# A two-layer decoder trunk: squares on ScalarE, earlier sums, another product order and spread loads in its MLPs

## The chip, the cores and the metric

The kernel runs on one core of a Trainium2 chip. The metric is the device time of one execution in microseconds (us), as the median of several runs. The profile is of one execution and has its own time, given below. Engines are named as in the profile: PE is TensorE's matmul, PEld its weight load, DVE is VectorE, ACT is ScalarE, POOL is GpSimd, SP (SPq for its queue) is SyncE, which issues the DMAs.

## The reference

One sequence of 512 positions, width 1024, two layers. Layer 0 mixes with a gated spatial unit and latent attention (the even mixer), layer 1 with gated linear attention (the odd mixer). The change is in the MLP, which both layers have:

```python
def sqrelu_mlp(x, w1, w2):
    return jnp.square(jax.nn.relu(x @ w1)) @ w2
# per layer, with d = 1024 and D_FF = 4096, everything float32
x = layer_norm(ALPHA * x + mixer(x), ln1_g[layer], ln1_b[layer])
x = layer_norm(ALPHA * x + sqrelu_mlp(x, w_ff1[layer], w_ff2[layer]), ln2_g[layer], ln2_b[layer])
```

## The kernel before

Each float32 operand of a matmul is held as two fp32r parts: `hi` is a cast by ACT, `lo` is what is left, a subtraction by DVE (`split`, L163 to L165). A product is three matmuls: hi by hi, hi by lo, lo by hi.

The MLP is `ff`. Its hidden width of 4096 is cut into eight groups of 2 x 256 columns (the group number is `g`, NG = 8). Group 0 is computed by eight plain block products (`plain`). Groups 1 to 7 use Strassen's scheme in Winograd's form: seven products of half-size blocks (`product`, named P1, p3, p5, p7, p6, P2, p4 in the order in which they run), with sums of blocks of x (s1 to s4, made once per layer in `x_sums`) and sums of blocks of w1 (t1 to t4, made for every group by `sum1`). A product has 24 matmuls of 256 columns.

The results of the seven products are combined by DVE (V, X and the blocks C11, C12, C21, C22; the table of steps L483 to L489), and each block passes `relu2`: relu and square by ACT, then twice DVE, then it lies in `hq[g]` as `hh` and `hl`. The second matrix is applied by chunk (`ff2_half`, chunk c takes `hq[c]`): eight halves, each with 12 matmuls of 512 columns, and each added into `XN` by DVE (`add_half`, L208). The last two chunks, 6 and 7, are the closing (`close_blocks` in layer 0, `close_final` in layer 1), which also does the layer norm; in layer 0 `norms` transposes a finished block of x (`block_T`, L194) while the next is computed.

The order on PE is: group 0, chunk 0, groups 1 and 2 one behind the other, chunk 1, group 3, chunk 2, and so on to group 7, then the closing. PE and DVE run their instructions in the order in which the program writes them (`manual_schedule`, `in_order`). The order on ACT and on SP is made by the framework's scheduler when the kernel is built.

Weights come in the order of the list `wseq`. `upto(n)` issues the loads and then the splits and sums ("terms") of all entries before place n. Ahead of each product and each half it runs a few places in front of what PE needs. Buffers that matter: `cr` (two, raw blocks B11 and B12, in which t1, t2, t4 and t3 are summed in place), `xk` (one, which holds the transposed x of the second half of the positions until its sums are made, and then B22 and B21 of a group), `raw` (three, for w2 and the next mixer's weights), six PSUM banks taken in turn, of which a group takes five and a half of a chunk one.

After the last group the next mixer's first weights are loaded: `prefetch` is `load_v0`, four granules (L129 to L140: a DMA, a cast by ACT, a subtraction by DVE at L138).

Of the kernel before, what the change touches and what calls it, by code (L numbers as in the profile page):

```python
# [12 lines left out]
F32 = mybir.dt.float32  # L13
F32R = mybir.dt.float32r
I32 = mybir.dt.int32
U8 = mybir.dt.uint8
AF = mybir.ActivationFunctionType
ALU = mybir.AluOpType

P = 128  # L20
D = 1024
# [82 lines left out]
def trunk(ctx: ExitStack, tc: tile.TileContext, a: dict, out: bass.AP):  # L104
    nc = tc.nc
# [19 lines left out]
    def bank(name, tag=None):  # L125
        tag = tag or next(cycle)
        return ps.tile([P, 512], F32, tag=tag, name=name, bufs=BANKS[tag])

    def granule(src, kb, cols, pool=wp, raw=None):  # L129

        n = kb * cols
        if raw is None:
            raw = wp.tile([P, WG], F32, tag="raw", name="raw", bufs=3)
        hi = pool.tile([P, WG], F32R, tag="whi", name="whi")
        lo = pool.tile([P, WG], F32R, tag="wlo", name="wlo")
        nc.sync.dma_start(raw[:, :n].rearrange("p (k c) -> p k c", k=kb), src.rearrange("(k p) c -> p k c", p=P))
        nc.scalar.copy(hi[:, :n], raw[:, :n])  # L137
        nc.vector.tensor_tensor(lo[:, :n], raw[:, :n], hi[:, :n].bitcast(F32), ALU.subtract)  # L138
        v = lambda x: x[:, :n].rearrange("p (k c) -> p k c", k=kb)
        return v(hi), v(lo)  # L140
# [14 lines left out]
    def granules(w, r0, rows, kb, cols, pool=wp):  # L155
        return [granule(w[r:r + kb * P, cols], kb, cols.stop - cols.start, pool) for r in range(r0, r0 + rows, kb * P)]
# [6 lines left out]
    def split(hi, lo, src):  # L163
        nc.scalar.copy(hi, src)  # L164
        nc.vector.tensor_tensor(lo, src, hi.bitcast(F32), ALU.subtract)  # L165
# [113 lines left out]
    HALF_S, HK_, GF = S // 2, KD // 2, 2 * P  # L279
# [4 lines left out]
    def ff(layer, hp, fp, xp, out_proj, prefetch):  # L284

        w1, w2 = a["w_ff1"][layer], a["w_ff2"][layer]
# [5 lines left out]
        ops = {"A11": (XH[:, lo_k, lo_t], XL[:, lo_k, lo_t]), "A12": (XH[:, hi_k, lo_t], XL[:, hi_k, lo_t]),  # L292
               "A22": (XH[:, hi_k, hi_t], XL[:, hi_k, hi_t]), "s1": (XH[:, lo_k, hi_t], XL[:, lo_k, hi_t])}
        xr, kept = {}, []
        ops["A21"] = ops["s1"]

        def operand(n, t, src, which=(0, 1)):
            h, l = (z[:, :, (t % 2) * P:(t % 2 + 1) * P] for z in ops[n])
            src = src.rearrange("p (k c) -> p k c", k=HK_)
            if 0 in which:  # L300
                nc.scalar.copy(h, src)
            if 1 in which:
                nc.vector.tensor_tensor(l, src, h.bitcast(F32), ALU.subtract)
# [17 lines left out]
        def x_lo(t):  # L321
            for h in range(2):
                operand(f"A{1 + t // 2}{1 + h}", t, xr[t, h], (1,))

        def x_sums():

            for n in ("s2", "s3", "s4"):
                ops[n] = (xp.tile([P, HK_, HALF_S], F32R, tag=n + "h", name="sh"),
                          xp.tile([P, HK_, HALF_S], F32R, tag=n + "l", name="sl"))
            for n, x, y, op in (("s3", (0, 0), (2, 0), ALU.subtract), ("s1", (2, 1), (2, 0), ALU.subtract),  # L330
                                ("s2", (0, 0), (2, 1), ALU.add), ("s4", (2, 1), (0, 1), ALU.subtract)):
                for t in range(2):
                    i, j = xr[x[0] + t, x[1]], xr[y[0] + t, y[1]]

                    to = i if n == "s3" else j
                    nc.vector.tensor_tensor(to, i, j, op)
                    operand(n, t, to)
                yield

        ff_T["now"] = x_T  # L340
# [6 lines left out]
        SUM = {"t1": ("B11", "B12"), "t3": ("B12", "B22"), "t2": ("t1", "B22"), "t4": ("t2", "B21")}  # L347

        def load1(g, n):

            for m in (n,) if g == 0 else {"B11": ("B11", "B12"), "B21": ("B21",), "B22": ("B22",)}.get(n, ()):
                if g == 0 and m != "B22":
                    raw = wp.tile([P, WG], F32, tag="raw", name="raw", bufs=3)
                elif g == 0 or m in ("B11", "B12"):
                    raw = xp.tile([P, WG], F32, tag="cr", name="cr", bufs=2)
                else:
                    if g not in kept2:
                        kept2[g] = xp.tile([P, 2, WG], F32, tag="xk", name="cr2")
                    raw = kept2[g][:, m == "B21"]
                raws[g, m] = raw  # L360
                nc.sync.dma_start(raw.rearrange("p (k c) -> p k c", k=HK_), w1v(*BLOCK[m], g))
# [32 lines left out]
        def load2(c, n, half):  # L394
            r = half * 2048 + c * GF
            raw = wp.tile([P, WG], F32, tag="raw", name="raw", bufs=3)
            nc.sync.dma_start(raw.rearrange("p (k c) -> p k c", k=2),
                              w2[r:r + GF, n * 512:(n + 1) * 512].rearrange("(k p) c -> p k c", p=P))
            raws["w2", c, n, half] = raw
# [13 lines left out]
        def scratch(g):  # L413

            return fp.tile([P, S], F32, name="r", **({"tag": "x", "bufs": 4} if g and next(turns) == "x" else {"tag": "q"}))

        def relu2(g, i, j, src, into=None):
            hh = hp.tile([P, 2, HALF_S], F32R, tag="hh", name="hh")
            hl = hp.tile([P, 2, HALF_S], F32R, tag="hl", name="hl")
            r = into if into is not None else scratch(g)  # L420
            f = lambda z: z.rearrange("p j t -> p (j t)")
            nc.scalar.activation(r, src, AF.Relu)
            nc.scalar.activation(f(hh), r, AF.Square)  # L423
            nc.vector.tensor_tensor(r, r, r, ALU.mult)  # L424
            nc.vector.tensor_tensor(f(hl), r, f(hh).bitcast(F32), ALU.subtract)  # L425
            hq[g][i, j] = hh, hl

        banks, state = {}, {}
# [12 lines left out]
        def plain(i, j, k):  # L441

            hq.setdefault(0, {})
            if k == 0:
                banks[0, i, j] = bank("f1")
            mul(banks[0, i, j], f"A{i + 1}{k + 1}", got_w[0, f"B{k + 1}{j + 1}"], k == 0)
            if k == 1:
                relu2(0, i, j, banks[0, i, j])
# [49 lines left out]
            add_half(t, n, acc, c == 0, None)  # L498


        LATER = ("P1", "p3", "p5", "p7", "p6", "P2", "p4")
        slots, wseq = [], []

        def put_group(g):
            slots.extend((g, n) for n in LATER)
            wseq.extend((g, n) for n in ("B11", "B22", "t1", "t3", "t2", "B21", "t4"))

        def put_chunk(c):
            slots.extend(("w2", c, n, t) for n in range(2) for t in range(NT))
# [7 lines left out]
            put_chunk(c)  # L517
        put_group(NG - 1)
        wseq += [("w2", c, n, h) for n in range(2) for c in (NG - 2, NG - 1) for h in range(2)]
        place = {w: i for i, w in enumerate(wseq)}  # L520
        at = {"load": 0, "terms": 0}
        LOADS, TERMS = 6, 6

        def upto(n, loads=None):

            while at["load"] < min(len(wseq), n + (LOADS if loads is None else loads)):
                w = wseq[at["load"]]
                at["load"] += 1
                (load2(*w[1:]) if w[0] == "w2" else load1(*w))
            while at["terms"] < min(len(wseq), n):  # L530
                w = wseq[at["terms"]]
                i = at["terms"]
                at["terms"] += 1
                if i + 1 < at["load"] and wseq[i + 1][0] != "w2":
                    sum1(*wseq[i + 1])
                (terms2(*w[1:]) if w[0] == "w2" else terms1(*w))

        todo = 0
        for _ in out_proj:
            todo += 1  # L540
            upto(min(todo, 4), 2)
        for n, (i, j, k) in enumerate(itertools.product(range(2), repeat=3)):
            upto(min(8, 4 + max(0, n - 1)))
            plain(i, j, k)
            if n == 1:
                x_T(NT - 1)
                x_lo(NT - 2)
                x_lo(NT - 1)
        sums = x_sums()
        for i, s in enumerate(slots):  # L550
            if s[0] == "w2":
                need = max(place["w2", s[1], s[2], 1], place["w2", s[1], s[2], 0])
# [8 lines left out]
            product(*s)  # L561
        upto(len(wseq))
        load_ln(a["ln2_g"][layer], a["ln2_b"][layer])
        got = prefetch() if prefetch else None

        def close_mm(t, n, acc, o, m, k0, k1):
            i, tc_ = t // 2, slice(t % 2 * P, (t % 2 + 1) * P)
# [17 lines left out]
        def close_blocks():  # L585
            stats, accs = new_stats(), {}

            def mm(t, n, k0, k1):
                if k0 == 0:
                    accs[n] = bank("f2")  # L590
                close_mm(t, n, accs[n], 0, 512, k0, k1)
                if k1 == KD:
                    add_half(t, n, accs[n], False, stats)

            for _ in norms(mm, stats):
                pass

        (close_final if layer == DEPTH - 1 else close_blocks)()
        return got
# [671 lines left out]
        return steps  # L1271

    v0_cols = 2 * C_HEADS * C_DK
    load_v0 = lambda: granules(a["w_in_odd"][0], 0, D, 2, slice(v0_cols, v0_cols + 512))
    with tc.tile_pool(name="m0", bufs=1) as mp:
        left = even_mixer(mp)
        with in_order():
# [47 lines left out]
```

## Time and profile before

| what | value |
|---|---|
| median of 3 runs (lowest, highest) | 1194.95 us (1194.72, 1195.26) |
| the profiled execution: its time | 1197.36 us |
| the profiled execution: its span, first to last instruction | 1195.7 us |
| PE busy | 1155.0 us, 97% of the span |
| PEld busy | 1006.0 us, 84% |
| DVE busy | 872.6 us, 73% |
| ACT busy | 482.5 us, 40% |
| mean granted TensorE clock | 0.987 |
| matmuls | 6888 |

The shares are means over the span, and matmuls are pipelined with modelled ends, so a PE that is busy at 97% can still lose time: a matmul that runs at the lower clock counts as busy. What an engine waited for is in the view of waits, and the length of a stage is read from where its first and last matmul lie.

### The profile page before, as it was taken

To read this page: it belongs to the slowest core of one execution; us is meant where nothing else is said; L and a number is where in the kernel's file an instruction comes from. 1 tells how busy PE (TensorE), PEld (TensorE's weight loads), DVE (VectorE), ACT (ScalarE), POOL (GpSimd) and SP (SyncE) were. 2 spreads that over 40 slices of the span, in tenths; PEclk is the share of its full clock that TensorE was granted. 3 is DMA by queue.
4 is the path that set the end of the run, shared out by engine and by line. 5 is a ranking of instruction groups with operands and counts; after the bars stand their busy time and mean duration, and the time that the engine had idled before them with its cause. 6 is when DMAs were issued, how large, how long until landed. Compare 5 with 4: busy or idle time off the path is not lost.

```text
span 1195.7 us, 17110 instructions
## 1 busy us (share of the span) xinstructions
PE 1155.0 (97%) x6888; PEld 1006.0 (84%) x6888; DVE 872.6 (73%) x1626; ACT 482.5 (40%) x737; POOL 4.5 (0%) x13
## 2 busy tenths in 40 slices
PE   8999999998899999997999999999998999999997
PEld 8988788888788998896878888778988889889976
DVE  6745697767788678667759559997687877876766
ACT  5466462324534443342155433442334434334420
POOL 0000000000000000000000000000000000000000
PEclk9999999999999999998999999999998999999999
DMA  7413142113341342224135312221223234313221
GB/s 246 138 36 113 46 142 88 53 54 106 106 138 56 124 142 66 75 89 137 40 108 141 89 51 74 71 70 54 71 85 112 77 117 141 123 36 124 71 71 53
DMA packets 84207, 111.68 MB, mean 93 GB/s; under 512 B 6080, under 2 KB 53056, under 8 KB 84128
## 3 DMA queue, kind: packets, MB, share of 16 engines
q1 hardware_dynamic: 84128, 110.59, 28.9%
q8 instruction: 54, 0.88, 0.3%
q14 instruction: 25, 0.20, 0.1%
HBM read 108.47 MB, written 2.10 MB: 92 GB/s over the span
## 4 chain that ended last, share of the span: by engine, by line
PE 80%; DVE 12%; ACT 4%; DMA 2%; issue 1%; SPq 0%; DVEq 0%; ACTq 0%
PE f L438 21%; PE f L161 8%; PE f L159 8%; PE f L160 8%; PE vg L159 3%; PE vg L160 2%; PE vg L161 2%; PE op L159 2%; PE op L161 2%; PE op L160 2%; DVE wlo L165 2%; DMA cr<-in_w_ff 1%; PE sc L808 1%; PE qk L159 1%; PE qk L160 1%; PE qk L161 1%
## 5 line engine op out<-in xcount | busy, mean ns | idle before, releaser
L161 PE MATMUL f<-whi,hl 128*128 128x512 f32 x448 | 178.3, 398 | 4.7 <-DVE hl L425 4.7
L159 PE MATMUL f<-whi,hh 128*128 128x512 f32 x448 | 178.2, 398 | 0.0
L160 PE MATMUL f<-wlo,hh 128*128 128x512 f32 x448 | 177.9, 397 | 0.0
L164 ACT CAST whi<-cr 128x1024 fp32r<-128x1024 f32 x98 | 100.8, 1048 | 172.0 <-DVE cr L368 146.7
L438 PE MATMUL f<-XH,whi 128*128 128x256 f32 x448 | 125.9, 281 | 2.3 <-DVE r L472 1.6
L438 PE MATMUL f<-XH,wlo 128*128 128x256 f32 x448 | 126.1, 282 | 0.7 <-DVE wlo L165 0.7
L438 PE MATMUL f<-XL,whi 128*128 128x256 f32 x448 | 125.8, 281 | 0.0
L165 DVE TENSOR_TENSOR wlo<-cr,whi 128x1024 fp32r<-128x1024 f32 x98 | 119.3, 1219 | 6.0 <-ACT whi L164 6.0
L438 PE MATMUL f<-sh,wlo 128*128 128x256 f32 x336 | 97.6, 290 | 11.0 <-DVE wlo L165 11.0
L161 PEld LDWEIGHTS f<-whi,hl 128*128 128x128 f32 x448 | 84.8, 189 | 26.0 <-DVE hl L425 5.6
L424 DVE TENSOR_TENSOR r<-r 128x512 f32<-128x512 f32 x64 | 44.2, 690 | 84.9 <-ACT hh L423 84.9
L160 PEld LDWEIGHTS f<-wlo,hh 128*128 128x128 f32 x448 | 85.0, 190 | 20.0
L159 PEld LDWEIGHTS f<-whi,hh 128*128 128x128 f32 x448 | 84.8, 189 | 19.6
L438 PE MATMUL f<-sh,whi 128*128 128x256 f32 x336 | 96.8, 288 | 0.2 <-ACT whi L164 0.2
L438 PE MATMUL f<-sl,whi 128*128 128x256 f32 x336 | 96.7, 288 | 0.0
L165 DVE TENSOR_TENSOR wlo<-raw,whi 128x1024 fp32r<-128x1024 f32 x56 | 66.8, 1221 | 32.0 <-ACT whi L164 32.0
L438 PEld LDWEIGHTS f<-XH,whi 128*128 128x128 f32 x448 | 84.4, 188 | 3.2 <-issue 1.8
L438 PEld LDWEIGHTS f<-XH,wlo 128*128 128x128 f32 x448 | 84.4, 188 | 1.1 <-DVE wlo L165 1.1
L438 PEld LDWEIGHTS f<-XL,whi 128*128 128x128 f32 x448 | 84.4, 188 | 0.5
L138 DVE TENSOR_TENSOR wlo<-raw,whi 128x1024 fp32r<-128x1024 f32 (+3 forms) x61 | 70.1, 1154 | 18.2 <-ACT whi L137 18.1
L208 DVE SCALAR_TENSOR_TENSOR XN<-XN,f 128x512 f32<-128x512 f32 (+1 forms) x113 | 72.3, 676 | 14.2 <-PE f L161 14.2
L164 ACT CAST whi<-raw 128x1024 fp32r<-128x1024 f32 x56 | 58.0, 1049 | 61.0 <-DMA raw<-in_w_ff 36.2
(270 smaller groups left out, 2544.1 us busy)
## 6 DMA issues: line engine op xcount, KB each, us to landing
raw<-in_w_ff SPq DMA_DIRECT2D x70, 512.0 KB, 4.6
cr<-in_w_ff SPq DMA_DIRECT2D x58, 512.0 KB, 4.6
raw<-in_w_in_odd SPq DMA_DIRECT2D x24, 512.0 KB, 3.9
XN<-in_x SPq DMA_DIRECT2D x16, 256.0 KB, 3.2
raw<-in_w_in_even SPq DMA_DIRECT2D x8, 512.0 KB, 3.7
raw<-in_w_out_even SPq DMA_DIRECT2D x8, 512.0 KB, 3.8
raw<-in_w_out_odd SPq DMA_DIRECT2D x8, 512.0 KB, 3.5
LB<-in_ln_b SPq DMA_DIRECT2D x4, 512.0 KB, 3.3
```

The source lines that it names most:

```text
L138: nc.vector.tensor_tensor(lo[:, :n], raw[:, :n], hi[:, :n].bitcast(F32), ALU.subtract)
L159: nc.tensor.matmul(acc, lh, rh, start=first, stop=False)
L160: nc.tensor.matmul(acc, lh, rl, start=False, stop=False)
L161: nc.tensor.matmul(acc, ll, rh, start=False, stop=last)
L164: nc.scalar.copy(hi, src)
L165: nc.vector.tensor_tensor(lo, src, hi.bitcast(F32), ALU.subtract)
L208: nc.vector.scalar_tensor_tensor(x, x, ALPHA if first else 1.0, acc, ALU.mult, ALU.add)
L424: nc.vector.tensor_tensor(r, r, r, ALU.mult)
L438: nc.tensor.matmul(d, l, r, start=first and j == k == i == 0, stop=j == 1 and k == HK_ - 1 and i == 2, skip_group_check=True)
L808: nc.tensor.matmul(sc[:, :N], qts[t][:B_QK, h, :], KT[:, h, :N], start=True, stop=True)
```

## The change

Four edits, all in `ff` but the last line.

- `relu2`: the square goes into the scratch buffer as float32 by ACT, and `split` follows (a cast by ACT, a subtraction by DVE). The multiplication by DVE is gone. There are 64 such blocks.
- `x_sums`: the eight sums of x run on DVE ahead of the fifth and sixth product of group 0 (four each). What is left for the first four halves of chunk 0 is, for each of s1, s3, s2 and s4, two casts by ACT and then two subtractions by DVE, where before each sum, cast and subtraction followed one another.
- The order of products is P1, p5, p7, p6, p3, P2, p4, and that of the weights B11, t1, t3, t2, B22, B21, t4. B22 is loaded at t1's place; t1 is summed when its own turn comes within a group, and the sum that follows still runs one place ahead. B11 of a group changes places with the w2 block before it.
- The four granules of `load_v0` become a list of single loads, and the closing of layer 0 issues one at each of its first four steps, that is after the halves and norms of the first two blocks, instead of all four ahead of it.

```diff
--- before.py
+++ after.py
@@ -324,17 +324,23 @@
 
         def x_sums():
 
-            for n in ("s2", "s3", "s4"):
-                ops[n] = (xp.tile([P, HK_, HALF_S], F32R, tag=n + "h", name="sh"),
-                          xp.tile([P, HK_, HALF_S], F32R, tag=n + "l", name="sl"))
-            for n, x, y, op in (("s3", (0, 0), (2, 0), ALU.subtract), ("s1", (2, 1), (2, 0), ALU.subtract),
-                                ("s2", (0, 0), (2, 1), ALU.add), ("s4", (2, 1), (0, 1), ALU.subtract)):
+            SUMS = (("s1", (2, 1), (2, 0), (2, 0)), ("s3", (0, 0), (2, 0), (0, 0)), ("s2", (0, 0), (2, 1), (2, 1)),
+                    ("s4", (2, 1), (0, 1), (0, 1)))
+            at = {}
+            for n, x, y, to in (SUMS[1], SUMS[0], *SUMS[2:]):
                 for t in range(2):
-                    i, j = xr[x[0] + t, x[1]], xr[y[0] + t, y[1]]
-
-                    to = i if n == "s3" else j
-                    nc.vector.tensor_tensor(to, i, j, op)
-                    operand(n, t, to)
+                    i, j, k = (xr[z[0] + t, z[1]] for z in (x, y, to))
+                    at[n, t] = k
+                    nc.vector.tensor_tensor(k, i, j, ALU.add if n == "s2" else ALU.subtract)
+                if n in ("s1", "s4"):
+                    yield
+            for n in ("s1", "s3", "s2", "s4"):
+                if n != "s1":
+                    ops[n] = (xp.tile([P, HK_, HALF_S], F32R, tag=n + "h", name="sh"),
+                              xp.tile([P, HK_, HALF_S], F32R, tag=n + "l", name="sl"))
+                for which in range(2):
+                    for t in range(2):
+                        operand(n, t, at[n, t], (which,))
                 yield
 
         ff_T["now"] = x_T
@@ -348,7 +354,7 @@
 
         def load1(g, n):
 
-            for m in (n,) if g == 0 else {"B11": ("B11", "B12"), "B21": ("B21",), "B22": ("B22",)}.get(n, ()):
+            for m in (n,) if g == 0 else {"B11": ("B11", "B12"), "B21": ("B21",), "t1": ("B22",)}.get(n, ()):
                 if g == 0 and m != "B22":
                     raw = wp.tile([P, WG], F32, tag="raw", name="raw", bufs=3)
                 elif g == 0 or m in ("B11", "B12"):
@@ -420,9 +426,8 @@
             r = into if into is not None else scratch(g)
             f = lambda z: z.rearrange("p j t -> p (j t)")
             nc.scalar.activation(r, src, AF.Relu)
-            nc.scalar.activation(f(hh), r, AF.Square)
-            nc.vector.tensor_tensor(r, r, r, ALU.mult)
-            nc.vector.tensor_tensor(f(hl), r, f(hh).bitcast(F32), ALU.subtract)
+            nc.scalar.activation(r, r, AF.Square)
+            split(f(hh), f(hl), r)
             hq[g][i, j] = hh, hl
 
         banks, state = {}, {}
@@ -498,12 +503,12 @@
             add_half(t, n, acc, c == 0, None)
 
 
-        LATER = ("P1", "p3", "p5", "p7", "p6", "P2", "p4")
+        LATER = ("P1", "p5", "p7", "p6", "p3", "P2", "p4")
         slots, wseq = [], []
 
         def put_group(g):
             slots.extend((g, n) for n in LATER)
-            wseq.extend((g, n) for n in ("B11", "B22", "t1", "t3", "t2", "B21", "t4"))
+            wseq.extend((g, n) for n in ("B11", "t1", "t3", "t2", "B22", "B21", "t4"))
 
         def put_chunk(c):
             slots.extend(("w2", c, n, t) for n in range(2) for t in range(NT))
@@ -517,6 +522,10 @@
             put_chunk(c)
         put_group(NG - 1)
         wseq += [("w2", c, n, h) for n in range(2) for c in (NG - 2, NG - 1) for h in range(2)]
+        for i, w in enumerate(wseq):
+            if w[0] != "w2" and w[1] == "B11" and i and wseq[i - 1][0] == "w2":
+
+                wseq[i - 1:i + 1] = wseq[i - 1:i + 1][::-1]
         place = {w: i for i, w in enumerate(wseq)}
         at = {"load": 0, "terms": 0}
         LOADS, TERMS = 6, 6
@@ -531,7 +540,9 @@
                 w = wseq[at["terms"]]
                 i = at["terms"]
                 at["terms"] += 1
-                if i + 1 < at["load"] and wseq[i + 1][0] != "w2":
+                if w[0] != "w2":
+                    sum1(*w)
+                if i + 1 < at["load"] and wseq[i + 1][1] in SUM and wseq[i + 1] != (w[0], "t1"):
                     sum1(*wseq[i + 1])
                 (terms2(*w[1:]) if w[0] == "w2" else terms1(*w))
 
@@ -539,14 +550,16 @@
         for _ in out_proj:
             todo += 1
             upto(min(todo, 4), 2)
+        sums = x_sums()
         for n, (i, j, k) in enumerate(itertools.product(range(2), repeat=3)):
             upto(min(8, 4 + max(0, n - 1)))
+            if n in (4, 5):
+                next(sums)
             plain(i, j, k)
             if n == 1:
                 x_T(NT - 1)
                 x_lo(NT - 2)
                 x_lo(NT - 1)
-        sums = x_sums()
         for i, s in enumerate(slots):
             if s[0] == "w2":
                 need = max(place["w2", s[1], s[2], 1], place["w2", s[1], s[2], 0])
@@ -561,7 +574,8 @@
             product(*s)
         upto(len(wseq))
         load_ln(a["ln2_g"][layer], a["ln2_b"][layer])
-        got = prefetch() if prefetch else None
+        got = []
+        ahead = iter(prefetch or ())
 
         def close_mm(t, n, acc, o, m, k0, k1):
             i, tc_ = t // 2, slice(t % 2 * P, (t % 2 + 1) * P)
@@ -593,7 +607,7 @@
                     add_half(t, n, accs[n], False, stats)
 
             for _ in norms(mm, stats):
-                pass
+                got.extend(load() for load in itertools.islice(ahead, 1))
 
         (close_final if layer == DEPTH - 1 else close_blocks)()
         return got
@@ -1271,7 +1285,7 @@
         return steps
 
     v0_cols = 2 * C_HEADS * C_DK
-    load_v0 = lambda: granules(a["w_in_odd"][0], 0, D, 2, slice(v0_cols, v0_cols + 512))
+    load_v0 = [lambda r=r: granule(a["w_in_odd"][0][r:r + 2 * P, v0_cols:v0_cols + 512], 2, 512) for r in range(0, D, 2 * P)]
     with tc.tile_pool(name="m0", bufs=1) as mp:
         left = even_mixer(mp)
         with in_order():
```

## Rows read from the trace of the kernel before

**Rows 1.** Waits of PE in the whole span: us in total, times, longest us.

```profile
PE f L438 <- DVE wlo L165: 11.7, 10, 2.7
PE f L161 <- DVE hl L425: 4.7, 2, 2.4
PE xt L194 <- DVE XN L223: 4.4, 1, 4.4
```

**Rows 2.** Stretches: length, then busy PE, PEld, DVE, ACT, POOL; PEclk, DMA share, GB/s.

```profile
271.00:322.50 51.50, 43.33 (x337) 41.77 (x336) 41.37 (x46) 24.07 (x30) 0.00 (x0) 0.97 0.36 111
322.50:344.90 22.40, 22.40 (x98) 18.06 (x97) 17.54 (x21) 9.47 (x12) 0.00 (x0) 1.00 0.20 68
344.90:364.80 19.90, 19.90 (x169) 19.86 (x168) 14.20 (x18) 9.06 (x12) 0.00 (x0) 1.00 0.56 186
534.00:591.80 57.80, 51.09 (x218) 41.35 (x217) 40.75 (x73) 13.96 (x19) 0.00 (x0) 0.91 0.29 89
877.00:927.50 50.50, 44.42 (x337) 43.17 (x336) 40.63 (x46) 24.35 (x30) 0.00 (x0) 0.93 0.38 121
1138.90:1154.10 15.20, 12.84 (x50) 10.12 (x49) 11.10 (x15) 5.09 (x7) 0.00 (x0) 0.89 0.31 105
```

**Rows 3.** Groups of DVE by line: xcount, busy us, mean ns, idle before.

```profile
L165 DVE TENSOR_TENSOR wlo<-cr,whi 128x1024 fp32r<-128x1024 f32 x98 | 119.3, 1219 | 6.0 <-ACT whi L164 6.0
...
L368 DVE TENSOR_TENSOR cr<-cr,cr 128x1024 f32<-128x1024 f32 x42 | 51.3, 1222 | 0.8
...
L424 DVE TENSOR_TENSOR r<-r 128x512 f32<-128x512 f32 x64 | 44.2, 690 | 84.9 <-ACT hh L423 84.9
```

**Rows 4.** The same view for ACT.

```profile
L423 ACT ACTIVATE hh<-r 128x512 fp32r<-128x512 f32 x64 | 38.8, 627 | 1.2
...
L301 ACT CAST sh<-xr 128x512 fp32r<-128x512 f32 x12 | 7.4, 620 | 22.4 <-DVE xr L336 22.4
```

**Rows 5.** Timeline of DVE, group 0 to group 1: start, us, idle in brackets.

```profile
244.43 0.69 DVE L424 TENSOR_TENSOR r<-r 128x512 f32<-128x512 f32 x1 [2.07 <-ACT hh L423]
...
250.19 0.69 DVE L424 TENSOR_TENSOR r<-r 128x512 f32<-128x512 f32 x1 [4.34 <-ACT hh L423]
...
257.46 0.69 DVE L303 TENSOR_TENSOR XL<-xr,XH 128x512 fp32r<-128x512 f32 x1 [0.69 <-ACT XH L301]
...
270.90 1.22 DVE L368 TENSOR_TENSOR cr<-cr 128x1024 f32<-128x1024 f32 x1
```

**Rows 6.** Timeline of DVE in group 7, the last of layer 0.

```profile
528.56 0.69 DVE L484 TENSOR_TENSOR LG<-f,LG 128x512 f32<-128x512 f32 x1 [3.51 <-PE f L438]
...
535.89 0.69 DVE L424 TENSOR_TENSOR r<-r 128x512 f32<-128x512 f32 x1 [1.33 <-ACT hh L423]
...
537.23 1.22 DVE L165 TENSOR_TENSOR ws<-raw,ws 128x1024 fp32r<-128x1024 f32 x1
538.37 0.68 DVE L424 TENSOR_TENSOR r<-r 128x512 f32<-128x512 f32 x1
539.09 0.69 DVE L425 TENSOR_TENSOR hl<-r,hh 128x512 fp32r<-128x512 f32 x1
```

**Rows 7.** Timeline of PE in the closing of layer 0.

```profile
539.83 0.50 PE L161 MATMUL f<-whi,hl 128*128 128x512 f32 x1 [2.36 <-DVE hl L425]
...
577.63 1.03 PE L194 MATMUL xt<-ident,XN 128*128 128x128 f32 x8
```

**Rows 8.** Timeline of DVE in the same closing.

```profile
550.87 1.23 DVE L138 TENSOR_TENSOR wlo<-raw,whi 128x1024 fp32r<-128x1024 f32 x1 [2.39 <-ACT whi L137]
...
556.08 0.68 DVE L208 SCALAR_TENSOR_TENSOR XN<-XN,f 128x512 f32<-128x512 f32 x1
...
562.16 1.28 DVE L223 SCALAR_TENSOR_TENSOR XN<-XN,ny,LB 128x1024 f32<-128x1024 f32 x1
```

**Rows 9.** Timeline of ACT at the end of group 5, layer 0.

```profile
458.09 0.60 ACT L422 ACTIVATE r<-f 128x512 f32<-128x512 f32 x1 [0.70 <-DVE f L480]
```

**Rows 10.** DMA issues: count, KB each, median us from issue to landing.

```profile
cr<-in_w_ff SPq DMA_DIRECT2D x58, 512.0 KB, 4.6
```

## The prediction, made before the result was known

> **What bounds the kernel now.** I read the waits of PE first. Three entries belong to the MLPs: PE waits 11.7 us for `wlo`, 4.7 us for `hl` and 4.4 us for `XN` [rows 1]. Then I measured stages. A group that stands between two chunks takes 19.9 us, a chunk 22.4 us, both with PE busy throughout at the full clock; they are the units: 2.84 us for a product, 0.233 us for a matmul of 512 columns [rows 2]. Against them four places lose time. Groups 1 and 2 should take 39.8 us and take 51.5 us in layer 0 and 50.5 us in layer 1 [rows 2]: 11.7 and 10.7 us lost. The closing of layer 0 has 192 matmuls, 44.8 us, and takes 57.8 us; three sets of transposes take at most 1.03 us each [rows 7], so 9.9 us are lost. The first two halves of the closing of layer 1, 48 matmuls, should take 11.2 us and take 15.2 us [rows 2]: 4.0 us lost. The granted clock in the four places is 0.97, 0.93, 0.91 and 0.89, where the undisturbed stages have 1.00 [rows 2]; the losses include that. Together 36.3 us, the most that this change can win; all of it is DVE being late, never ACT or a DMA alone.
>
> Why DVE is late is in its timeline. Ahead of chunk 0 it idles 2.07 and 4.34 us [rows 5]; then, in chunk 0, each sum of x, cast by ACT and subtraction follow one another, with 0.69 us of waiting each time, and only at 270.90, when PE starts group 1, does DVE come to t1 [rows 5]. Two groups then follow without a chunk between, and DVE cannot catch up.
>
> **The change, part by part.** The prices: a subtraction or sum of 1024 columns takes 1.22 us on DVE [rows 3] and the next starts 1.14 us after it [rows 6]; one of 512 columns 0.69 us [rows 3]; an ACT operation of 512 columns 0.62 to 0.63 us [rows 4].
>
> *Squares.* DVE loses 64 operations of 0.69 us, 44.2 us in all [rows 3]; ACT gains 64 casts of 0.62 us [rows 4], 40 us. But DVE runs in order and waits 84.9 us in total in front of the multiplication that goes [rows 3]. Now it waits for three ACT operations, where it waited for two: 1.33 us [rows 6] becomes 2.0 us, and what it saves is just that wait. Where the subtraction comes late anyway (C11) it saves its 0.7 us. So the edit alone is worth little on the path; nothing reads `hh` so soon that its cast 0.6 us later matters, except in the closing, counted below. I take the cast at 0.62 us; one of the same shape and types is in the rows, so this price has no bounds to keep.
>
> The Trainium skill ("ScalarE: Activation LUTs", Rules for kernel authors) speaks against this edit: a multiplication belongs on VectorE. At this shape the rows say otherwise, 0.627 us for a square on ACT against 0.690 us on DVE [rows 3, 4]. The page gives no factor for float32; were ACT to take twice DVE's time (an estimate), each chain would be 0.7 us longer, the gain about 6 us smaller. The rows price both operations, so I give this no chance of its own.
>
> *Sums of x.* Eight sums, at most 5.5 us, move into waits of 2.07 and 4.34 us [rows 5]; if that cover were gone they would delay the last block of group 0, which only the third half of chunk 0 reads. In chunk 0 there remain two subtractions and an addition into XN per half in each of the first four halves, some 2 us beside 2.8 us of PE. The buffer `xk` comes free after s2's subtractions, near 256, not after s4's sum, some 2 us ahead of 270.90; B22 lands 4.6 us [rows 10] later, at 261, when t3's sum wants it. SP holds every later load behind B22's, and all of these move up too. So by 271.0 DVE has B11, t1 and t3 done, where it had B11 alone.
>
> *The order, groups 1 and 2.* In the time of the old trace: p6, now the fourth product, ends at 282.4. V, X and C22's subtraction are done at 284.8, ACT's three operations give 286.8, `hl` 287.4, B11 of group 2 288.5, C12's subtraction 289.2, its wait and `hl` 291.8, sums of t1 and t3 and the split of t1 295.2. PE wants t1 at 293.7: it waits 1.5 us. C11, t2's sum and t3 end at 298.1, when PE comes to p7. C21 (0.7, 2.0, 0.6) and t2 end at 302.5; PE wants t2 at 300.9: 1.6 us. B22 is in time. So 3.1 us remain of 11.7 and of 10.7: gains of 8.6 and 7.6 us. Bounds for what remains: nothing (DVE idles some 5 us before V and the framework may lay out ACT well), and 9.4 us with the first rival below.
>
> *The order, end of the last group.* The old closing waits for C11's `hl`: DVE comes to V at 528.56 and to C11 at 538.37, starts `hl` at 539.09 [rows 6], and PE, idle for 2.36 us, goes on at 539.83 [rows 7]; so it wanted it at 537.5. Now p6 ends 2.84 us sooner, at 525.5. V, X, C22 take DVE to 527.9, its wait and `hl` to 530.5, a w2 split 531.6, C12 534.9, a split 536.1, C11's `hl` 536.7: in time by 0.8 us. The next: C21 ends at 541.1 and the last two splits at 542.3 and 543.4, where PE wants them at 542.6 and 544.0. These margins are thin and a cast by ACT in between costs 1 us, so I leave 0.4 us of loss in each layer.
>
> *Granules.* Four subtractions at L138 stand ahead of the first addition, one waiting 2.39 us, and that addition comes at 556.08; the norm ends at 562.16 + 1.28 [rows 8], and PE's transposes wait for it 4.4 us [rows 1]. Now one granule stands there. From the first addition to the end of the norm it was 7.4 us [rows 8]; from 543.4 with a granule of 1.2 us between it ends at 552.0, and PE wants it at 555.0. The DMAs still need a free `raw`, but each is issued a half or more before its subtraction, against 4.6 us of landing [rows 10]. If a granule is late DVE has 3 us in hand. The odd mixer uses them 25 us later. So the closing of layer 0 wins 9.9 - 0.4 = 9.5 us, that of layer 1 4.0 - 0.4 = 3.6 us (it has no granules).
>
> The sum: 8.6 + 7.6 + 9.5 + 3.6 = 29.3 us. The profiled execution took 1197.36 us (span 1195.7 us), so 1168.1 us (span 1166.4 us); it lies 2.4 us above the median of the runs, so the median goes from 1194.95 to 1165.7 us.
>
> **The rivals.** First: the handshake eats the gain of groups 1 and 2. ACT's order is the framework's; if it puts a weight cast or two (about 1.1 us each by the same rate) into each of the three chains on DVE's path there (C22, C12, C21), DVE is 3.2 to 6.3 us later in each layer. For it: DVE already waits 84.9 us for `hh` [rows 3], and the chain is one operation longer. Against it: those casts mostly wait for sums that DVE does later. Taken at 6.3 us twice: 1178.3 us.
>
> Second: the closings keep their stalls. If the granules or C21's chain make DVE 5 us later there, the transposes wait 2 us again, the clock falls as before, and C11 is late: about half of 13.1 us stays lost, 1172.3 us.
>
> Third, the other side: PSUM. The six banks go round; the bank of C21 now is the fourth that the next chunk asks for, before it was the fifth. PE asks 8.4 us after the group ends (three halves), where it had 11.2 us. C21's relu ended at 458.69 [rows 9], 9.3 us after group 5 ended (364.8 and two rounds of 42.3 us, 449.4). By the new order V comes 8.5 us before the group's end, and V, X, C22, B11's split, C12, t1's sum, a w2 split, C11, t3's sum, t1's split, C21 and its relu take 15.8 us at these prices: 7.3 us after the end, a margin of 1.1 us. Beyond that every delay is paid six times in each layer; from 3.5 us of it the kernel is slower than before (12 x 2.4 us against 29.3 us). At 4 us: 1200.5 us. Against it: the margin is computed with every wait at its full length, and in the old group 3 and chunk 1 PE is busy throughout [rows 2].
>
> Fourth: no change. If the odd mixer and the tails were set by DMAs, time won before would be waited out. But PE waits for no DMA in any entry of weight, so 1195 us has little for it.
>
> **How the numbers follow.** Forecast 0.68, first rival 0.15, second 0.08, third 0.05, fourth 0.04. The first two are faster too: faster 0.91, same 0.04, slower 0.05; 0.2% (2.4 us) is about what runs of this kernel can tell from no change. The forecast's own range is 1158.7 us (all 36.3 us won) to 1173 us (7 us more left). For 8 in 10, the lower end stays, rounded to 1158 us, and the upper takes in the second rival and most of the first: 1180 us.
>
> **What would show it.** The multiplication is gone and 64 casts stand in its place; t1's sum lies before PE starts group 1; groups 1 and 2 take 40 to 46 us in both layers; no wait for C11's `hl` over 1 us and none of the transposes for XN; clock 1.00 in these stretches; chunks still 22.4 us. The prediction is wrong if chunks 1 to 5 are longer than that (PSUM), if groups 1 and 2 stay near 50 us (ACT's order), or if a wait turns up at the start of the odd mixer.

## The result, and the profile after

| what | before | after |
|---|---|---|
| median of 4 runs each, on the same chip (lowest, highest) | 1195.11 us (1194.72, 1196.62) | 1175.06 us (1173.22, 1176.52) |
| ratio, with its 95% interval | | 0.9829 [0.981, 0.9848] |
| span of the profiled execution | 1195.7 us | 1174.2 us |
| mean granted TensorE clock | 0.987 | 0.994 |

The change wins 20 us, where the forecast was 29.3 us. The page of the profile after, first its shares (busy us, share, instructions), then a group of instructions (busy us, mean ns, idle before):

```profile
PE 1146.1 (98%) x6888; PEld 999.5 (85%) x6888; DVE 825.3 (70%) x1562; ACT 520.3 (44%) x801; POOL 4.6 (0%) x13
...
L165 DVE TENSOR_TENSOR hl<-r,hh 128x512 fp32r<-128x512 f32 x64 | 44.2, 690 | 109.8 <-ACT hh L164 109.8
```

The 64 multiplications of [rows 3] are gone from DVE (x1562, before x1626) and ACT has 64 operations more (x801, before x737). DVE's wait did not go with them: the 84.9 us in front of the multiplication are now 109.8 us in front of the subtraction.

The same view of waits as [rows 1], after (us in total, times, longest):

```profile
PE f L443 <- DVE wlo L165: 6.1, 4, 2.3
...
PE f L160 <- DVE ws L165: 1.6, 2, 0.8
PE f L160 <- DVE wlo L165: 1.5, 2, 0.8
...
PE f L443 <- ACT whi L164: 0.8, 2, 0.4
...
PE f L161 <- DVE hl L165: 0.5, 2, 0.3
```

L443 is the old L438. The wait of the products for `wlo` fell from 11.7 to 6.1 us, that for `hl` from 4.7 to 0.5 us, and the transposes' 4.4 us for `XN` are gone. Two small entries are new: halves that wait for `wlo` or `ws` (L160).

The same stretches as in [rows 2]: groups 1 and 2, chunk 1, group 3 and the closing of layer 0, then groups 1 and 2 and the closing's first two halves of layer 1 (length, busy PE, PEld, DVE, ACT, POOL; clock, DMA share, GB/s):

```profile
271.00:316.60 45.60, 42.12 (x337) 41.48 (x336) 28.57 (x31) 23.10 (x32) 0.00 (x0) 0.96 0.31 98
316.60:340.00 23.40, 22.67 (x98) 17.98 (x97) 19.44 (x23) 9.76 (x13) 0.00 (x0) 1.00 0.28 90
340.00:359.90 19.90, 19.90 (x169) 19.89 (x168) 11.63 (x14) 10.91 (x15) 0.00 (x0) 1.00 0.45 147
528.70:577.20 48.50, 47.46 (x218) 38.37 (x217) 37.68 (x69) 15.44 (x21) 0.00 (x0) 1.00 0.37 116
862.40:907.90 45.50, 42.02 (x337) 41.39 (x336) 28.61 (x31) 23.14 (x32) 0.00 (x0) 0.96 0.32 99
1119.90:1132.60 12.70, 11.61 (x50) 8.88 (x49) 8.48 (x11) 6.75 (x9) 0.00 (x0) 1.00 0.45 164
```

Against [rows 2] groups 1 and 2 won 5.9 and 5.0 us, the closing of layer 0 9.3 us, that of layer 1 2.5 us measured to its last matmul (48.8 to 46.3 us). Chunk 1 lost 1.0 us, and 1.1 us in layer 1. That makes 20.6 us of the span's 21.5 us; the rest is spread over chunks that came out 0.1 us shorter. No other stage moved.

### The profile page after: what moved, and what is told of

Same layout as the page of the kernel before. It is cut to its first block, busy times and chain, and to the rows that moved or that the text cites. A ratio compares the mean times of both kernels' runs of the same rounds, so it can differ in the third digit from the quotient of the medians.

```text
span 1174.2 us, 17121 instructions
## 1 busy us (share of the span) xinstructions
PE 1146.1 (98%) x6888; PEld 999.5 (85%) x6888; DVE 825.3 (70%) x1562; ACT 520.3 (44%) x801; POOL 4.6 (0%) x13
## 4 chain that ended last, share of the span: by engine, by line
PE 86%; DVE 7%; ACT 5%; issue 1%; DMA 0%; SPq 0%; DVEq 0%; ACTq 0%
PE f L443 24%; PE f L160 9%; PE f L161 9%; PE f L159 9%; PE vg L159 3%; PE vg L161 3%; PE vg L160 3%; PE op L159 3%; PE op L161 2%; PE op L160 2%; PE sc L822 1%; PE qk L159 1%; DVE wlo L165 1%; PE qk L160 1%; PE qk L161 1%; PE o L844 1%
## 5 line engine op out<-in xcount | busy, mean ns | idle before, releaser
L160 PE MATMUL f<-wlo,hh 128*128 128x512 f32 x448 | 177.0, 395 | 1.5 <-DVE wlo L165 1.5
L443 PE MATMUL f<-XH,wlo 128*128 128x256 f32 x448 | 126.1, 281 | 1.6 <-DVE wlo L165 1.6
L443 PE MATMUL f<-XH,whi 128*128 128x256 f32 x448 | 126.1, 281 | 0.8 <-ACT whi L164 0.8
L443 PE MATMUL f<-XL,whi 128*128 128x256 f32 x448 | 125.8, 281 | 0.0
L165 DVE TENSOR_TENSOR hl<-r,hh 128x512 fp32r<-128x512 f32 x64 | 44.2, 690 | 109.8 <-ACT hh L164 109.8
L160 PEld LDWEIGHTS f<-wlo,hh 128*128 128x128 f32 x448 | 84.3, 188 | 21.5 <-DVE wlo L165 2.4
L443 PE MATMUL f<-sh,wlo 128*128 128x256 f32 x336 | 96.2, 286 | 4.5 <-DVE wlo L165 4.5
L443 PE MATMUL f<-sh,whi 128*128 128x256 f32 x336 | 95.8, 285 | 0.0
L443 PE MATMUL f<-sl,whi 128*128 128x256 f32 x336 | 95.8, 285 | 0.0
L443 PEld LDWEIGHTS f<-XH,wlo 128*128 128x128 f32 x448 | 84.4, 188 | 2.0 <-DVE wlo L165 2.0
L443 PEld LDWEIGHTS f<-XH,whi 128*128 128x128 f32 x448 | 84.4, 188 | 1.8 <-ACT whi L164 1.2
L443 PEld LDWEIGHTS f<-XL,whi 128*128 128x128 f32 x448 | 84.4, 188 | 0.5
L137 ACT CAST whi<-raw 128x1024 fp32r<-128x1024 f32 (+3 forms) x61 | 60.2, 991 | 50.0 <-DMA raw<-in_w_in_odd 22.1
```

Source lines behind the costliest of these rows:

```text
L160: nc.tensor.matmul(acc, lh, rl, start=False, stop=False)
L443: nc.tensor.matmul(d, l, r, start=first and j == k == i == 0, stop=j == 1 and k == HK_ - 1 and i == 2, skip_group_check=True)
```

## The experiments

In each, the question is the length of the four stages. The table holds them for all runs, worked out as in the forecast, from the first matmul of one stage to the first of the next (the closing of layer 1 to its last matmul). A ratio is to the runs of the kernel before that were made beside each, whose median lay between 1195.1 and 1196.8 us.

| kernel | median us | ratio [95%] | chunk 0 | groups 1+2 | chunk 1 | closing |
|---|---|---|---|---|---|---|
| before, layer 0 / 1 | 1195.11 | 1 | 22.3 / 22.3 | 51.5 / 50.5 | 22.4 / 22.3 | 57.8 / 48.8 |
| after | 1175.06 | 0.9829 [0.981, 0.9848] | 22.4 / 22.3 | 45.6 / 45.5 | 23.4 / 23.4 | 48.5 / 46.3 |
| squares alone | 1194.07 | 0.9988 [0.9979, 0.9998] | 22.3 / 22.3 | 50.1 / 49.1 | 22.6 / 24.0 | 56.1 / 47.9 |
| sums of x alone | 1189.08 | 0.995 [0.9934, 0.9967] | 22.3 / 22.3 | 47.4 / 47.5 | 22.3 / 22.3 | 57.1 / 48.7 |
| order alone | 1200.53 | 1.0037 [1.0024, 1.005] | 29.4 / 30.2 | 44.9 / 46.4 | 24.0 / 23.9 | 56.0 / 47.2 |
| granules alone | 1188.13 | 0.9937 [0.9922, 0.9952] | 22.3 / 22.3 | 51.7 / 49.7 | 22.3 / 22.4 | 50.7 / 48.5 |
| after without order | 1179.96 | 0.9868 [0.9853, 0.9882] | 22.3 / 22.3 | 46.3 / 46.9 | 22.4 / 22.3 | 50.2 / 47.9 |
| after without squares | 1179.41 | 0.9861 [0.9846, 0.9876] | 22.3 / 22.3 | 46.4 / 46.3 | 23.9 / 24.0 | 49.5 / 47.3 |
| after without sums | 1189.52 | 0.995 [0.9935, 0.9965] | 29.9 / 30.7 | 45.6 / 44.1 | 23.4 / 23.4 | 48.5 / 46.7 |
| order without exchange | 1187.58 | 0.9934 [0.9915, 0.9952] | 22.4 / 22.3 | 49.3 / 48.6 | 22.3 / 22.7 | 55.8 / 47.2 |
| after, w2 split first | 1172.69 | 0.9808 [0.979, 0.9826] | 22.3 / 22.3 | 45.5 / 45.6 | 22.4 / 22.4 | 48.6 / 46.5 |
| after, splits ahead | 1168.64 | 0.9774 [0.976, 0.9789] | 22.3 / 22.3 | 44.0 / 42.6 | 22.5 / 22.3 | 48.6 / 46.3 |
| both, ahead for group 1 | 1164.7 | 0.9745 [0.9729, 0.9761] | 22.4 / 22.3 | 41.5 / 41.5 | 22.3 / 22.3 | 48.6 / 46.6 |

The stages are the safer measure. The profiled executions already differ by up to 3.3 us before PE comes to its first `kv` matmul (between 44.31 and 47.62 us), a stretch that no edit touches, while the odd mixer between the two MLPs takes 238.5 us in all of them. So two medians some 2 us apart settle little.

**One part alone on the kernel before.** Squares:

```diff
-            nc.scalar.activation(f(hh), r, AF.Square)
-            nc.vector.tensor_tensor(r, r, r, ALU.mult)
-            nc.vector.tensor_tensor(f(hl), r, f(hh).bitcast(F32), ALU.subtract)
+            nc.scalar.activation(r, r, AF.Square)
+            split(f(hh), f(hl), r)
```

> The kernel before with the square on ACT alone. Theory (DVE waits for ACT in order, so a wait takes the place of the multiplication): groups 1 and 2 shorten by 1 to 2 us in each layer, the closings by 0.7 us, together -2 to -5 us. Rival (DVE's amount of work sets groups 1 and 2): 8 multiplications of 0.69 us less there in each layer, 5.5 us and the clock with them, -11 to -14 us in all.

Sums of x (with the new body of `x_sums`):

```diff
+        sums = x_sums()
         for n, (i, j, k) in enumerate(itertools.product(range(2), repeat=3)):
             upto(min(8, 4 + max(0, n - 1)))
+            if n in (4, 5):
+                next(sums)
...
```

> The kernel before with the sums of x inside group 0 alone. Theory (DVE starts group 1 late because of the ping-pong in chunk 0): groups 1 and 2 go from 51.5 and 50.5 us to 44 to 47 us, -9 to -14 us in all. Rival (the order of the weights is what keeps PE waiting there): under 3 us in all. The closings stay at 57.8 and 15.2 us in either.

Order (with the loads, sums and exchange that belong to it):

```diff
...
-        LATER = ("P1", "p3", "p5", "p7", "p6", "P2", "p4")
+        LATER = ("P1", "p5", "p7", "p6", "p3", "P2", "p4")
...
-            wseq.extend((g, n) for n in ("B11", "B22", "t1", "t3", "t2", "B21", "t4"))
+            wseq.extend((g, n) for n in ("B11", "t1", "t3", "t2", "B22", "B21", "t4"))
...
+        for i, w in enumerate(wseq):
+            if w[0] != "w2" and w[1] == "B11" and i and wseq[i - 1][0] == "w2":
+                wseq[i - 1:i + 1] = wseq[i - 1:i + 1][::-1]
...
```

> The kernel before with the order of products and weights alone. Theory: the wait for C11's hl ahead of both closings goes from 2.4 us to under 1 us, and with it the clock's fall, -3 to -7 us; groups 1 and 2 change by less than 3 us each, since DVE is as late as before. Rival (order decides there): groups 1 and 2 under 47 us, more than -10 us in all. The first chunk behind group 2 gets 1 us longer in either, if that is the sum of t1 ahead of its last w2 split.

Granules:

```diff
-        got = prefetch() if prefetch else None
+        got = []
+        ahead = iter(prefetch or ())
...
-                pass
+                got.extend(load() for load in itertools.islice(ahead, 1))
...
```

> The kernel before with the granules spread alone. Theory: only the closing of layer 0 changes, from 57.8 us to 50 to 51.5 us (no wait of the transposes for XN, the wait for hl stays), -6 to -8 us. Rival (the norm is late because DVE is behind anyway): the wait for XN stays above 2 us and the gain below 3 us.

Against their own median before, 1195.41 us, the four measure -1.3, -6.3, +5.1 and -7.3 us, -9.8 us in all, where together they give -20. Three of the four expectations missed. The squares win 1.4 us in groups 1 and 2 of each layer and 1.7 and 0.9 us in the closings, but chunk 1 of layer 1 loses 1.7 us; the stages add up to 3.3 us, the median shows 1.3 us. The sums stop at 47.4 and 47.5 us in groups 1 and 2, just short of the 44 to 47 us, and at -6.3 us in all, short of the -9 to -14 us. With the order, the wait for C11's `hl` falls to 1.1 us (expected under 1 us) and the closings win 1.8 and 1.6 us, but neither its theory nor its rival had a loss. So the parts interact, and the order is the one that needs another: alone it makes the kernel slower. The reason stands in the timelines of DVE and PE in chunk 0 with the order alone (start, us, idle in brackets; the lines of each engine in its own fence):

```profile
262.87 0.68 DVE L336 TENSOR_TENSOR xr<-xr,xr 128x512 f32<-128x512 f32 x1
264.24 0.69 DVE L303 TENSOR_TENSOR sl<-xr,sh 128x512 fp32r<-128x512 f32 x1 [0.68 <-ACT sh L301]
264.85 1.22 DVE L368 TENSOR_TENSOR cr<-cr 128x1024 f32<-128x1024 f32 x1
265.99 1.22 DVE L165 TENSOR_TENSOR wlo<-raw,whi 128x1024 fp32r<-128x1024 f32 x1
```

```profile
267.26 0.80 PE L160 MATMUL f<-wlo,hh 128*128 128x512 f32 x1 [5.31 <-DVE wlo L165]
```

The exchange of B11 with the w2 block before it sets chunk 0's last w2 split behind B11 and t1. With the sums of x still in chunk 0, DVE comes to that split at 265.99, and PE has waited 5.31 us for it. Chunk 0 takes 29.4 us instead of 22.3. Groups 1 and 2 of layer 0 win 6.6 us beside it, nearly what chunk 0 pays; in layer 1 it is 4.1 us for 7.9 us.

Granules alone give 7.1 us in the closing of layer 0 and at most 0.8 us in any other stage, as was expected of them.

**One part undone in the kernel after.** The same lines, backwards.

> The changed kernel with the old order of products and weights. Theory (the order pays only in the closings, and costs 1 us in chunk 1): groups 1 and 2 stay at 45 to 47 us, chunk 1 goes back from 23.4 to 22.4 us, the closings get 0.7 and 1.6 us longer by the wait for C11's hl; in all within 3 us of the changed kernel. Rival (the order spreads DVE's work in the groups, as the prediction had it): groups 1 and 2 at 48 us or more and the closings over 50 us, +8 us or more.

> The changed kernel with the multiplication back on DVE. Theory (a wait for ACT takes the place of the multiplication): +2 to +5 us, most of it in groups 1 and 2. Rival (DVE's amount of work decides): groups 1 and 2 longer by 5 us in each layer, +11 us or more.

> The changed kernel with the sums of x back in chunk 0. Theory (sums and order belong together: the exchange of B11 is only harmless once the sums are out of chunk 0): chunk 0 at 28 to 30 us in both layers, groups 1 and 2 at 43 to 46 us, +8 to +14 us against the changed kernel. Rival (with DVE relieved of the squares the sums no longer matter): under +5 us, chunk 0 at 22 to 24 us.

The order is worth 4.9 us within the whole: 3.3 us in the closings, 2.1 us in groups 1 and 2, and about 0.1 us in each of the later chunks, while each chunk 1 is 1.0 us shorter without it. That is more than my theory's 3 us and less than the rival's 8 us. The squares are worth 4.4 us in the whole, 1.3 us alone. The two intervals of that 4.4 us touch, but the stages add up to 4.7 us: 2.0 in the closings, 1.6 in groups 1 and 2 and 1.1 in chunk 1, where most of it had been expected in groups 1 and 2. Without the sums the kernel is 14.5 us slower, where 8 to 14 us were expected, and chunk 0 again takes 29.9 and 30.7 us: with the exchange and without the sums it loses 7 to 8 us, whether the squares and granules are in or not.

**The order without the exchange**, on the kernel before: the diff of the order without the three lines of the loop over `wseq`.

> The kernel before with the new order of products and weights, but B11 not exchanged with the w2 block before it. Theory (the order alone was slower because the exchange puts the last w2 split of chunk 0 behind the sums of x on DVE): chunk 0 goes from 29 to 30 us back to 22 to 23 us, chunk 1 from 24 to 22.4 us; groups 1 and 2 take back some of it and come to 48 to 51 us; in all 3 to 8 us faster than the order with the exchange. Rival (DVE is just late in chunk 0): chunk 0 stays above 26 us.

Chunk 0 is back at 22.4 us and the time 12 to 13 us below that with the exchange (by the ratios and by the medians), more than the 3 to 8 us expected. So the price of the order alone is the exchange, not the order of products: without it the order alone wins 7.6 us. Whether the kernel after would be faster without the exchange was not run. The exchange gives something too: groups 1 and 2 take 44.9 us with it and 49.3 us here, where t1's sum comes at 269.26, 22.2 us into chunk 0; with the exchange it came at 264.85, 15.9 us into it, and PE, held up in chunk 0, began group 1 only 13.5 us after it.

**The w2 split ahead of the next sum**, on the kernel after, for chunk 1:

```diff
+                if w[0] == "w2":
+                    terms2(*w[1:])
                 if i + 1 < at["load"] and wseq[i + 1][1] in SUM and wseq[i + 1] != (w[0], "t1"):
                     sum1(*wseq[i + 1])
-                (terms2(*w[1:]) if w[0] == "w2" else terms1(*w))
+                if w[0] != "w2":
+                    terms1(*w)
```

> The changed kernel with the last w2 split of a chunk issued ahead of the sum of t1 that now stands before it. Theory: chunk 1 goes from 23.4 to 22.4 us in both layers and nothing else moves, -2 us. Rival (DVE is late there for the whole of group 2, whatever stands before the split): chunk 1 stays above 23 us.

The timeline of DVE in chunk 1 shows what was mended; first the kernel after, then this one:

```profile
327.95 1.22 DVE L374 TENSOR_TENSOR cr<-cr 128x1024 f32<-128x1024 f32 x1
329.08 1.22 DVE L165 TENSOR_TENSOR wlo<-raw,whi 128x1024 fp32r<-128x1024 f32 x1
```

```profile
326.20 0.68 DVE L208 SCALAR_TENSOR_TENSOR XN<-XN,f 128x512 f32<-128x512 f32 x1
326.80 1.22 DVE L165 TENSOR_TENSOR wlo<-raw,whi 128x1024 fp32r<-128x1024 f32 x1
327.93 1.22 DVE L374 TENSOR_TENSOR cr<-cr 128x1024 f32<-128x1024 f32 x1
```

In the kernel after t1's sum of group 3 (L374) runs ahead of the last w2 split that chunk 1 needs, and the half waits 0.73 us for it. With the two exchanged chunk 1 is 22.4 us in both layers, and groups 1 and 2 are as before: the 1.0 us of chunk 1 is this and nothing else. In the median it is 2.4 us; the intervals of the two ratios overlap, so the stages show it and the medians only agree.

**Splits further ahead**, on the kernel after, for the waits for t1 and t2 in groups 1 and 2:

```diff
-                    upto(max(need + 1, 8 + i // 2))
+                    upto(max(need + 1, 8 + 2 * i // 3))
...
-            upto(place[s[0], PRODUCTS[s[1]][1]] + 1 + min(TERMS, 2 + s[0]))
+            upto(place[s[0], PRODUCTS[s[1]][1]] + 1 + min(TERMS, 3 + s[0]))
```

> The changed kernel with splits and sums one place further ahead in groups 1 and 2 and up to one place in chunk 0, so that DVE does them while it waits for p6. Theory (PE's waits for t1 and t2 of group 2 come from DVE's idle 5 us before p6): groups 1 and 2 go from 45.6 to 41 to 44 us, -3 to -9 us in all. Rival (the chains of C22, C12 and C21 with ACT set the pace, not the place of the splits): groups 1 and 2 stay above 44.5 us.

The second line also moves group 3 one place. Both waits are gone from the view of waits and the groups take 44.0 and 42.6 us. What is left has another cause; PE at the end of group 2, and DVE ahead of it:

```profile
309.24 0.36 PE L443 MATMUL f<-XH,whi 128*128 128x256 f32 x1 [2.18 <-DVE r L477]
```

```profile
302.35 2.43 DVE L165 TENSOR_TENSOR wlo<-cr,whi 128x1024 fp32r<-128x1024 f32 x2
304.69 2.35 DVE L165 TENSOR_TENSOR wlo<-raw,whi 128x1024 fp32r<-128x1024 f32 x2
306.96 0.68 DVE L489 TENSOR_TENSOR LG<-f,LG 128x512 f32<-128x512 f32 x1
307.68 0.69 DVE L490 TENSOR_TENSOR LB<-LG,f 128x512 f32<-128x512 f32 x1
308.40 0.69 DVE L477 TENSOR_TENSOR r<-LB,f 128x512 f32<-128x512 f32 x1
```

The product p4 adds into the bank that C22's subtraction (L477) reads, and has to wait for it. DVE comes to V, X and C22 of group 2 only at 306.96, because four splits issued further ahead stand before them. So the look-ahead has two ends: too short and the split is late, too long and the combination is.

Layer 1 has the same stall at the same place, and yet its groups take 1.4 us less. The stretches behind the two stalls differ in the granted clock, 0.52 in layer 0 and 1.00 in layer 1 (fields as above):

```profile
898.65 0.36 PE L443 MATMUL f<-XH,whi 128*128 128x256 f32 x1 [2.18 <-DVE r L477]
```

```profile
310.20:313.60 3.40, 3.40 (x19) 3.40 (x19) 0.00 (x0) 1.36 (x2) 0.00 (x0) 0.52 0.92 330
899.60:903.00 3.40, 3.40 (x25) 3.14 (x25) 0.00 (x0) 1.99 (x3) 0.00 (x0) 1.00 0.89 316
```

**Ahead for group 1 alone**, with the w2 split first and the first of the two lines above; group 2 keeps the old number of places:

```diff
-            upto(place[s[0], PRODUCTS[s[1]][1]] + 1 + min(TERMS, 2 + s[0]))
+            upto(place[s[0], PRODUCTS[s[1]][1]] + 1 + min(TERMS, 4 if s[0] == 1 else 2 + s[0]))
```

> The changed kernel with the last w2 split ahead of t1's sum and with splits one place further ahead in chunk 0 and group 1 only. Theory (in the lookahead run the splits issued ahead of V in group 2 made PE wait 2.2 us for the bank that C22's subtraction still had to read, and lowered the clock): groups 1 and 2 go to 40 to 42 us, chunk 1 to 22.4 us, 1164 to 1168 us in all, faster than the lookahead run. Rival (that wait only moves to t1 and t2 of group 2): groups 1 and 2 at 43 us or more, no faster than the lookahead run.

```profile
308.33 0.36 PE L443 MATMUL f<-XH,whi 128*128 128x256 f32 x1 [1.04 <-DVE r L477]
```

The same wait is 1.04 us now, and the two stages of this kernel read:

```profile
269.80:311.30 41.50, 40.41 (x338) 40.00 (x337) 27.86 (x31) 22.78 (x31) 0.00 (x0) 1.00 0.30 94
311.30:333.60 22.30, 22.30 (x98) 18.08 (x98) 18.31 (x21) 10.33 (x13) 0.00 (x0) 1.00 0.32 109
```

Groups 1 and 2 take 41.5 us in both layers, 1.7 us above the 39.8 us of two groups, at the full clock. The kernel takes 1164.7 us, 10 us less than the kernel after, and is the fastest of all that ran; its interval only touches that of the one with splits further ahead, so the step between these two is less sure than the other.

## Why the prediction came out as it did

**Groups 1 and 2: the term "3.1 us remain" was too small; 5.8 and 5.7 us remain.** The order of events was right, and its times nearly so. PE's waits in the kernel after, layer 0:

```profile
294.33 0.39 PE L443 MATMUL f<-XH,whi 128*128 128x256 f32 x1 [0.42 <-ACT whi L164]
...
295.64 0.39 PE L443 MATMUL f<-XH,wlo 128*128 128x256 f32 x1 [0.81 <-DVE wlo L165]
...
303.88 0.39 PE L443 MATMUL f<-sh,wlo 128*128 128x256 f32 x1 [2.25 <-DVE wlo L165]
```

PE goes on with t1 at 295.64 (forecast 295.2) after 0.42 and 0.81 us of waiting (forecast 1.5), and with t2 at 303.88 (forecast 302.5) after 2.25 us (forecast 1.6). The waits make 3.5 us of idle time, and 4.3 us counted from one matmul's start to the next, against 3.1. An error of about the same size is what follows the second one, which the sum left out: the granted clock in the stretch behind it.

```profile
304.50:308.00 3.50, 3.50 (x19) 3.50 (x19) 3.50 (x4) 1.88 (x2) 0.00 (x0) 0.51 0.00 0
```

PE is busy throughout and its clock is 0.51 there, the lower of its two levels (1.2 of 2.4 GHz): the 17 matmuls from 304.45 to 307.98 take 3.5 us, where at the 0.118 us of the full clock they take 2.0, so 1.5 us are lost. With the 4.3 us of the waits that is the 5.8 us; in layer 1 it is 4.4 and 1.3 us. The run with splits further ahead shows the clock's part by itself: the stall of 2.18 us stands in both layers, the clock fell behind it in layer 0 alone, and groups 1 and 2 took 44.0 and 42.6 us. After the stall of 1.04 us at the same place, in the last run, it fell in neither layer. So the slower stretch may follow a stall of that length or not; that it followed in both layers of the kernel after is partly bad luck. The forecast priced the old falls as recovered and no new one; [rows 2] had a clock of 0.97 and 0.93 in these stretches, so a term of its own was there to be read.

The 1.4 us by which t2 is late are partly the first rival, in small. ACT in C21's chain, and DVE behind it:

```profile
299.26 0.59 ACT L428 ACTIVATE r<-f 128x512 f32<-128x512 f32 x1
299.75 1.04 ACT L164 CAST whi<-cr 128x1024 fp32r<-128x1024 f32 x1
300.68 0.63 ACT L429 ACTIVATE r<-r 128x512 f32<-128x512 f32 x1
301.35 0.62 ACT L164 CAST hh<-r 128x512 fp32r<-128x512 f32 x1
```

```profile
286.74 0.69 DVE L165 TENSOR_TENSOR hl<-r,hh 128x512 fp32r<-128x512 f32 x1 [2.01 <-ACT hh L164]
...
302.00 0.69 DVE L165 TENSOR_TENSOR hl<-r,hh 128x512 fp32r<-128x512 f32 x1 [2.93 <-ACT hh L164]
```

A weight's cast stands between relu and square, and DVE waits 2.93 us where it waits 2.01 us, as forecast, without one. That is 0.9 us in one of the three chains, not one or two casts in each. No run moved this cast alone.

**The squares: right in kind.** The wait takes the place of the multiplication, 2.01 us for the forecast's 2.0, and alone the edit is worth 1.3 us, "little on the path". In the whole it is worth 4.4 us. A square takes ACT 632 ns after the change, the multiplication took DVE 690 ns [rows 3]. So the rule of the Trainium skill that was weighed, a multiplication on VectorE and not on ScalarE ("ScalarE: Activation LUTs", Rules for kernel authors), does not hold for this shape and type: putting the multiplication back made the kernel slower.

**The sums of x: right.** In the kernel after the sum of t1 runs in chunk 0, at 256.23, B22's load is issued behind s2's subtractions, at 256.38 (forecast 256), and t3's sum runs at 260.90 (forecast 261). PE loses nothing in chunk 0 by the moved work. This part carries the gain of groups 1 and 2: alone it gives 4.1 and 3.0 us there, while the order adds 0.7 and 1.4 us to the whole, by the run that undoes it. The forecast costed the two as one and could not say so.

**Chunks "still 22.4": wrong for chunk 1, by 1.0 us in each layer.** The exchange has no term of its own in the sum: the split that it sets back was not followed to the half that reads it. The same step without the sums costs chunk 0 7 us.

**The closings: the mechanism right, the 0.4 us left in each too small.** The granules now stand between the additions. DVE in the closing of layer 0, beside [rows 8]:

```profile
539.73 0.68 DVE L208 SCALAR_TENSOR_TENSOR XN<-XN,f 128x512 f32<-128x512 f32 x1
...
541.05 1.21 DVE L138 TENSOR_TENSOR wlo<-raw,whi 128x1024 fp32r<-128x1024 f32 x1
...
546.95 1.28 DVE L223 SCALAR_TENSOR_TENSOR XN<-XN,ny,LB 128x1024 f32<-128x1024 f32 x1
```

From the first addition to the norm's end it takes 8.5 us, one granule and all (forecast 8.6), and PE's transposes stand at 551.05 without a wait, 2.8 us after it (forecast 3.0). C11's `hl`, which had kept PE waiting 2.36 us [rows 7], is late by 0.27 us where 0.8 us in hand was forecast, and the split behind C21 by 0.77 us:

```profile
532.38 0.50 PE L161 MATMUL f<-whi,hl 128*128 128x512 f32 x1 [0.27 <-DVE hl L165]
538.73 0.50 PE L160 MATMUL f<-ws,hh 128*128 128x512 f32 x1 [0.77 <-DVE ws L165]
```

ACT has here, too, a weight's cast (535.27, 1.03 us) in C21's chain. So 1.0 us is waited for the forecast's 0.4; layer 1 shows the same two waits and wins 2.5 us of the 3.6. The second rival did not occur: the clock is 1.00 in both closings.

**The other rivals.** PSUM: C21's relu ends 7.5 us after the end of group 5 (forecast 7.3), inside the 8.4 us that PE leaves, and no wait of PE for a bank shows in the kernel after. With the splits further ahead it does show, once: one half of chunk 2 waits 0.15 us for that relu, and the chunk takes 22.8 us. The margin is as thin as it was worked out. No change: no load took over the bound.

In sum the span fell short of its forecast by 7.8 us: 5.3 us in groups 1 and 2 (of it some 2.8 us the clock), 2.1 us in chunk 1, 1.3 us in the closings, less 0.9 us that other stages were shorter. The median of 1175.06 us lies 2 us above the forecast's own range (1158.7 to 1173 us) and inside the wider one (up to 1180 us), which was drawn for rivals of which the second did not occur and the first only in part: that it holds the result is partly luck.

## What to carry to other kernels

A stall of the matmul engine is priced with what follows it: read the granted clock behind the stalls of the kernel before, and add the slower stretch behind each stall that the forecast leaves as a term with two values, here 0 and about 1.4 us. When an edit sets one step ahead of another in an engine's order, follow the one that is set back to its reader; the order with the exchange was worth 4.9 us where another edit had emptied that stretch, and cost 5.1 us where it had not. And a look-ahead has two ends: more of it cured the late split and made the late combination, until it was set by group (p4's wait for a bank that DVE had still to read).

## What the hardware showed that was not expected

In one kernel, the one with splits further ahead, the same stall of 2.18 us was followed by some 3 us of matmuls at half clock (0.21 us each instead of 0.118) in layer 0 and by none in layer 1. In the MLPs of all thirteen traces PE has 27 waits of 1.0 to 1.7 us, and one of them is followed within 4.5 us by a stretch at the lower clock. Of the 31 waits of 1.75 to 2.6 us 24 are, and the stretch cost 1.1 to 1.5 us each time; of the 13 longer waits all are. What decides between two waits of one length was not measured.
